# Gate-build look-ahead of a ten-stage fp32 network: one step per four tokens, 45 units ahead, three loads ahead earlier, and a step between query and scores

## Chip, cores and metric

The kernel runs on one core of a Trainium2 chip. The metric is the device time of one execution, in microseconds, as the median of several runs. A profile of one further execution supplies the trace.

## The reference, cut to what matters

Ten stages run one after the other on 256 tokens of width 1024, all in fp32. Two of them (`p0` and `p1`, one in each layer of the first block) are a routed feed-forward with 16,384 experts per layer. Both are the same code; the change is in them alone.

```python
q = (xb @ w_q).reshape(n, 8, 2, 128)                    # 8 heads, two half-queries each
s = einsum('nhpc,pkc->nhpk', q, subkeys)                # scores against 128 keys per half
sv, si = top_k(s, 16)
cand = sv[:, :, 0, :, None] + sv[:, :, 1, None, :]      # 16 x 16 candidates
fv, fi = top_k(cand.reshape(n, 8, 256), 16)
eid = ...                                               # si0 * 128 + si1 of the 16 winners
gw = softmax(fv)
act = gelu(einsum('nhkd,nd->nhk', u_tab[eid], xb))
y = einsum('nhkd' , (gw * act), v_tab[eid])             # sum over heads and winners
```

The other eight stages (an mLSTM mixer, an RG-LRU mixer, four gated feed-forwards, an S5 mixer, a convolution mixer) are not touched.

## The kernel before

**Dense instead of gathered.** The kernel does not gather expert rows. It multiplies all 256 tokens with all 16,384 rows of `u` and of `v`, and puts a gate matrix in between that is zero for experts a token did not choose. `u` and `v` are cut into 64 units of 256 experts (1 MB each). Every fp32 product is three fp32r matmuls (high x high, low x high, high x low), so each unit is split after its load: ScalarE copies the high part (line 217, tile `uwh` or `vwh`), VectorE subtracts to get the low part (line 218, `uwl` or `vwl`).

**Stages of a peer block.** In the order of the program:

- *Route* (`route`): projects the queries (256 columns of `w_q` per head), scores them (`psc`, line 909, copied to `sc`), takes the top 16 twice on VectorE (lines 661 to 672), decodes the winners (`decode`) and turns weights and indices into the rows `sel` (`selection`).
- *Gate build* (`build_gates`): makes the gate matrix for eight tokens at a time, `n` = 0 to 31. VectorE writes four one-hot tiles `oh` of 128x1024 (lines 1026 and 1028), TensorE multiplies them in two groups of eight small matmuls into `pG` (lines 1039 and 1040, one group per four tokens), ScalarE copies each group into `stg` (line 1042), and every 16 tokens a 1 MB store takes `stg` to `gd` in DRAM (line 1045, ScalarE's queue; `stg` has two buffers). Below, a *half* is one of the 64 passes of its inner loop: four tokens, two one-hots, one group.
- *Drain*: the rest of the look-ahead, with nothing else beside it.
- *y loop*: 64 passes over the units of `v`; each loads and splits a unit of `v`, multiplies the activations by the gates (`gt`, loaded from `gd`), splits them (`pch`, `pcl`), and runs 24 matmuls of 512 columns into the four banks `py`. From pass `LOOK - 3` on, each pass also computes one more unit of `u`.

**The look-ahead.** Activations gelu(u x) don't depend on the routing, so `ahead()` is a generator that works on units of `u` while route and gate build go on. One *step* is a `next(gen)`: 12 matmuls of 256 columns into `pP`, and at every second step the split of half a unit that the matmuls reach four steps later (128x1024 elements on ScalarE, then the same on VectorE). Four steps are one unit; a gelu ends it. `LOOK` units are made this way. The first 15 stay in SBUF (`lact`); those after them are spilled to DRAM (`ad`, line 733, 0.25 MB each, on SyncE's queue) and recalled in the y loop (line 741), except the last three (`pact`).

Where the steps go is written out by hand. `tick(cost, rate)` in `route` adds cost times rate to a credit and runs a step for each whole credit. In `build_gates` each half adds `RATE[3]` and runs at most one step:

```python
one_hot(n + 1, coming, (2 * g, 2 * g + 1))
credit += RATE[3]
if credit >= 1.0:
    credit -= 1.0
    next(gen, None)
gates(n, oh, g)
```

Ahead of the loop come four one-hots for the first eight tokens with three steps between them. By the credits, 97 steps are run before the loop, 57 in it, and the rest of the 160 in the drain.

**Order.** In `route` the instructions of TensorE, VectorE and ScalarE keep the order of the program (`in_order`); in `build_gates` SyncE's do too. Each engine's queue is then fixed, and an instruction that waits holds up those behind it. Loads and spills share SyncE's queue. `depth[0]` says how many units past the current one have been issued for loading: 1 in `route`, 3 in the build (`DEP`); three `raw` buffers hold them.

**Query and scores.** `project(h)` is a generator that `route` advances twice per pass of `candidates`: two empty advances, the first half of the projection (24 matmuls), the second half with the copy to `pq` (line 888, ScalarE), one more empty advance, then the scores `psc`, which read `pq`.

Of the kernel before, what the change touches and what calls it, by code (L numbers as in the profile page):

```python
# [35 lines left out]
S5S = ("00001111",) + ("01010101",) * 3  # L36
S5O = "s0 s1; s2 s3|y0 y1; t0 t1 s4 s5|w2 g0 g1 w3 y2 y3; t2 t3 s6 s7|g2 g3 y4 y5; t4 t5|y6 g4 y7 t6 g5 t7 g6 g7"
DEP = (1, 3)
RATE = (2.0, 0.66, 1.33, 0.9)
SPN = 3  # L40
LPN = 1
IOR = ("tensor","vector","scalar")
# [1 line left out]
NX = (4, 2, 2, 2)  # L44
FILL = (3,) * 20
LATE = (3, 4)
LOOK = 40
TAIL = (9, 1)
PARTS = (4, 4) + (2,) * 40
MAGIC = 12582912.0  # L50
# [7 lines left out]
class K:  # L58
# [615 lines left out]
    def peer(self, x, xt, nxt, i):  # L674
        nc, a, tc = self.nc, self.a, self.tc
        HOLD, KEEP = 15, 3
        with ExitStack() as st:
# [3 lines left out]
            gd = self.dram.tile([P, 16, P, 16], F32, name=f"gd{i}")  # L681
            ad = self.dram.tile([P, max(1, LOOK - KEEP - HOLD), 2, S], F32, name=f"ad{i}")
            sel = [lpool.tile([P, S], F16, name=f"sel{j}") for j in range(4)]
# [31 lines left out]
            def u_mm(q, s):  # L715
# [8 lines left out]
                if s == 3:  # L724
                    if q < HOLD:
                        ac = lpool.tile([P, 2, S], F32, name="lact", tag="lact", bufs=HOLD)
                    elif q < LOOK - KEEP:
                        ac = top.tile([P, 2, S], F32, name="spact", tag="spact", bufs=2)
                    else:
                        ac = top.tile([P, 2, S], F32, name="pact", tag="pact", bufs=KEEP + 2)  # L730
                    nc.scalar.activation(ac, ps.rearrange("p (k s) -> p k s", k=2), AF.Gelu)
                    if HOLD <= q < LOOK - KEEP:
                        nc.sync.dma_start(ad[:, q - HOLD], ac)
# [4 lines left out]
            def recall(q):  # L738
                if HOLD <= q < LOOK - KEEP:
                    acts[q] = top.tile([P, 2, S], F32, name="spact", tag="spact", bufs=2)  # L740
                    nc.sync.dma_start(acts[q], ad[:, q - HOLD])

            def v_load(q):
# [4 lines left out]
                if q == 62:  # L748
                    raw = slots["r"][0].rearrange("p (k n) -> p k n", k=2)
                    vst[q] = [raw[:, k:k + 1] for k in range(2)]  # L750
                elif q > LOOK - KEEP:
                    vst[q] = [self.res.tile([P, 1, D], F32, tag="v", name="vraw", bufs=2) for _ in range(2)]
# [36 lines left out]
            def ahead():  # L789
                u_load(0)  # L790
                for s in range(4):
                    u_split(0, s)
                n = 0
                for q in range(LOOK):
                    while n < min(q + depth[0], LOOK):
                        n += 1
                        u_load(n)
                    for s in range(4):
                        u_split(q + 1, s)
                        u_mm(q, s)  # L800
                        yield

            depth = [DEP[0]]
            gen = ahead()
            with tc.tile_pool(name="route", bufs=1) as pool:
                self.route(pool, xt, i, sel, gen)
            with tc.tile_pool(name="build", bufs=1) as pool:
                depth[0] = DEP[1]
                with self.in_order(True, None, IOB):
# [43 lines left out]
            nxt.load()  # L853
            return self.residual_ln(x, banks, g, b, nxt)

    def route(self, pool, xt, i, sel, gen):
        nc, a = self.nc, self.a
        sk = pool.tile([P, 2, P], F32, name="sk")
        nc.sync.dma_start(sk, a["peer_subkeys"][i].rearrange("h k c -> k h c"))
# [14 lines left out]
        def tick(cost, rate):  # L874
            credit[0] += cost * rate
            while credit[0] >= 1.0:
                credit[0] -= 1.0
                next(gen, None)

        def weights(h):  # L880
            if h < 8:
                raw = self.ring.tile([P, 2048], F32, tag="raw", name="raw").rearrange("p (k n) -> p k n", k=8)
                nc.sync.dma_start(raw, a["peer_w_q"][i][:, h * 256:h * 256 + 256].rearrange("(p k) c -> p k c", k=8))
                units[h] = raw

        def query(h, ps):
            heads[h] = pool.tile([P, 2, S], F32, name="pq", tag="pq", bufs=2)
            nc.scalar.activation(heads[h], ps.rearrange("p (f s) -> p f s", f=2), AF.Copy)

        def project(h):  # L890
            if h >= 8:
                return
            yield
            yield
            if h >= 2:
                w = units.pop(h)
                ps = self.mmb()
                for f in range(2):
                    self.feat(ps[:, f * S:(f + 1) * S], w, f * P, (f + 1) * P, xt)
                    if f == 0:  # L900
                        yield
                query(h, ps)
            yield
            yield
            qT = heads.pop(h)
            pss = self.acc("psc")
            for t in range(2):
                for f in range(2):
                    nc.tensor.matmul(pss[:, (2 * t + f) * P:(2 * t + f + 1) * P], qT[:, f, t * P:(t + 1) * P],
                                     skT[:, f, :], start=True, stop=True)  # L910
            sc[h] = pool.tile([P, 4, P], F32, name="sc", tag="sc", bufs=2)
            nc.scalar.activation(sc[h], pss.rearrange("p (f s) -> p f s", f=4), AF.Copy)

        def candidates(h):
            for t in range(2):
                self.top16(*((sc[h][:, 2 * t + f, :], sv[t][:, h, f, :], si[t][:, h, f, :]) for f in range(2)))
                yield 2.0
            cds = []
            for t in range(2):
                cd = pool.tile([P, 112], F32, name="cd", tag="cd", bufs=2)  # L920
                for c0, a0, na, nb in ((0, 0, 4, 16), (64, 4, 12, 4)):
                    nc.vector.tensor_tensor(cd[:, c0:c0 + na * nb].rearrange("p (a b) -> p a b", a=na),
                                            sv[t][:, h, 0, a0:a0 + na, None].to_broadcast([P, na, nb]),
                                            sv[t][:, h, 1, None, 0:nb].to_broadcast([P, na, nb]), ALU.add)
                cds.append((cd, fv[t][:, h, :], fp[t][:, h, :]))
            yield 0.6
            self.top16(*cds)
            yield 2.0
# [36 lines left out]
        for _ in project(0):  # L965
            tick(1.0, RATE[0])
        with self.in_order(True, None, IOR):
            late = iter(())
            for h in range(8):
                ahead = project(h + 1)  # L970
                for n, cost in enumerate(candidates(h)):
                    next(ahead, None)
                    if n == LPN:
                        weights(h + 2)
                    tick(cost, RATE[1])
                    next(ahead, None)
                    if n == SPN and h + 2 in units:
                        units[h + 2] = self.split(units[h + 2], 8, 256)
                        tick(2.2, RATE[1])
                    if h >= 4:  # L980
                        d = next(late, None)
                        if d is not None:
                            tick(d, RATE[2])
                for _ in ahead:
                    pass
                if h == 3:
                    late = decode(slice(0, 4))
            for late in (late, decode(slice(4, 8))):
                for cost in late:
                    tick(cost, RATE[2])  # L990
            self.selection(pool, mk, gen, sel, fv, ix)
# [25 lines left out]
    def build_gates(self, pool, sel, gd, gen):  # L1017
# [3 lines left out]
        def one_hot(n, oh, js):  # L1021
            for j in js if n < 32 else ():
                o = pool.tile([P, 4, P, 2], F16, name=f"oh{j}", tag=f"oh{j}", bufs=2)
                sc = sel[j][:, n * 8:n * 8 + 8].rearrange("p (g t) -> p g t", g=4)[:, :, None, :].to_broadcast([P, 4, P, 2])
                if j < 2:
                    nc.vector.tensor_tensor(o, self.iota2[:, None].to_broadcast([P, 4, P, 2]), sc, ALU.is_equal)
                else:
                    nc.vector.tensor_tensor(o, oh[1], sc, ALU.mult)
                oh.append(o)
# [23 lines left out]
        for n in range(32):  # L1053
            for g in range(2):
# [3 lines that stand above are left out]
# [707 lines left out]
```

## Time and profile before

| what | value |
|---|---|
| median of 3 runs | 3032.01 us (3028.15 to 3034.11) |
| profiled execution | 3031.37 us |
| its span in the trace | 3029.7 us |
| TensorE matmul busy | 2939.7 us (97%) |
| TensorE weight load busy | 2684.8 us (89%) |
| VectorE busy | 2052.3 us (68%) |
| ScalarE busy | 1571.9 us (52%) |
| mean DMA rate | 205 GB/s |

Busy shares are averages over all ten stages. The page's matmul ends are modelled, so a busy TensorE is not one at its peak; idle time of an engine counts only where it holds up the one that sets the end. Times of the trace are counted from the start of the span.

### The profile page before, as it was taken

How to read it: one execution, taken by the hardware profiler on the slowest of the kernel's cores; microseconds unless marked ns; L12 is line 12 of the kernel's file. 1: busy time of each engine (PE TensorE's matmuls, PEld its weight loads, DVE VectorE, ACT ScalarE, POOL GpSimd, SP SyncE). 2: the span in 40 equal slices, each digit the busy share in tenths (PEclk: the TensorE clock that was granted, in tenths of full speed). 3: DMA queues.
4: the chain of work that ended last, by engine and by line, in shares of the span. 5: the costliest groups of instructions: out<-in, count | busy, mean ns of one | idle time of the engine just before them, and what ended most of it. 6: DMA issues, size and time to landing. Idle time of an engine off the chain costs nothing. (4 is left out here: it accounts for less than half of the span.)

```text
span 3029.7 us, 48905 instructions
## 1 busy us (share of the span) xinstructions
PE 2939.7 (97%) x20062; PEld 2684.8 (89%) x20062; DVE 2052.3 (68%) x3516; ACT 1571.9 (52%) x2180; POOL 10.9 (0%) x18
## 2 busy tenths in 40 slices
PE   9999999999999999989999999999899999999999
PEld 8899898888999889989888899899888999998898
DVE  5678897565555778989666555677776455479554
ACT  4544486444444664468444444456835454466544
POOL 0000000000000000000000000000000000000000
PEclk9999999999999999999999999999999999999999
DMA  7355489785665644568877565566864565552353
GB/s 235 126 169 181 171 293 311 239 286 188 222 210 181 216 155 154 181 226 298 271 268 257 182 222 197 194 200 225 297 226 165 180 206 178 173 169 98 126 192 128
DMA packets 332220, 620.70 MB, mean 205 GB/s; under 512 B 32444, under 2 KB 243292, under 8 KB 310493
## 3 DMA queue, kind: packets, MB, share of 16 engines
q1 hardware_dynamic: 327389, 584.03, 58.0%
q10 hardware_dynamic: 4608, 33.56, 2.7%
q8 instruction: 157, 2.57, 0.3%
q14 instruction: 66, 0.54, 0.1%
HBM read 557.77 MB, written 59.77 MB: 204 GB/s over the span
## 5 line engine op out<-in xcount | busy, mean ns | idle before, releaser
L218 DVE TENSOR_TENSOR wl<-raw,wh 128x1024 fp32r<-128x1024 f32 (+1 forms) x440 | 481.1, 1123 | 165.1 <-ACT wh L217 164.1
L217 ACT ACTIVATE wh<-raw 128x1024 fp32r<-128x1024 f32 (+1 forms) x440 | 411.4, 974 | 172.8 <-PE py L154 47.9
L152 PE MATMUL pP<-xth,uwh 128*128 128x256 f32 x1664 | 485.2, 292 | 1.0 <-ACT uwh L217 1.0
L154 PE MATMUL pP<-xth,uwl 128*128 128x256 f32 x1664 | 473.0, 284 | 1.8 <-DVE uwl L218 1.8
L153 PE MATMUL pP<-xtl,uwh 128*128 128x256 f32 x1664 | 472.7, 284 | 0.0
L152 PE MATMUL pf<-xth,wh 128*128 128x256 f32 x1280 | 363.1, 284 | 1.3 <-ACT wh L217 1.3
L154 PE MATMUL pf<-xth,wl 128*128 128x256 f32 x1280 | 362.9, 284 | 0.0
L153 PE MATMUL pf<-xtl,wh 128*128 128x256 f32 x1280 | 362.6, 283 | 0.0
L154 PEld LDWEIGHTS pP<-xth,uwl 128*128 128x128 f32 x1664 | 320.7, 193 | 2.7 <-DVE uwl L218 2.6
L152 PEld LDWEIGHTS pP<-xth,uwh 128*128 128x128 f32 x1664 | 320.9, 193 | 2.2 <-ACT uwh L217 1.2
L153 PEld LDWEIGHTS pP<-xtl,uwh 128*128 128x128 f32 x1664 | 321.3, 193 | 1.1
L152 PE MATMUL py<-vwh,pch 128*128 128x512 f32 x800 | 315.9, 395 | 2.0 <-ACT pch L217 2.0
L153 PE MATMUL py<-vwl,pch 128*128 128x512 f32 x800 | 315.8, 395 | 1.5 <-DVE vwl L218 1.4
L154 PE MATMUL py<-vwh,pcl 128*128 128x512 f32 x800 | 315.2, 395 | 0.0
L152 PEld LDWEIGHTS pf<-xth,wh 128*128 128x128 f32 x1280 | 245.3, 192 | 4.6 <-ACT wh L217 1.6
L153 PEld LDWEIGHTS pf<-xtl,wh 128*128 128x128 f32 x1280 | 245.5, 192 | 2.3
L218 DVE TENSOR_TENSOR uwl<-raw,uwh 128x1024 fp32r<-128x1024 f32 x164 | 199.4, 1220 | 69.9 <-ACT uwh L217 68.0
L154 PEld LDWEIGHTS pf<-xth,wl 128*128 128x128 f32 x1280 | 245.5, 192 | 0.6 <-DVE wl L218 0.4
L218 DVE TENSOR_TENSOR vwl<-raw,vwh 128x2048 fp32r<-128x2048 f32 x76 | 174.2, 2292 | 82.7 <-ACT vwh L217 82.5
L217 ACT ACTIVATE uwh<-raw 128x1024 fp32r<-128x1024 f32 x164 | 169.9, 1057 | 39.6 <-DMA raw<-in_peer_u 14.4
L152 PEld LDWEIGHTS py<-vwh,pch 128*128 128x128 f32 x800 | 150.8, 188 | 36.8 <-ACT pch L217 2.8
L153 PEld LDWEIGHTS py<-vwl,pch 128*128 128x128 f32 x800 | 150.7, 188 | 36.4 <-DVE vwl L218 2.3
(558 smaller groups left out, 6536.0 us busy)
## 6 DMA issues: line engine op xcount, KB each, us to landing
raw<-in_ffn_w SPq DMA_DIRECT2D x132, 1024.0 KB, 5.3
raw<-in_peer_u SPq DMA_DIRECT2D x82, 1024.0 KB, 5.5
raw<-in_peer_v SPq DMA_DIRECT2D x76, 1024.0 KB, 5.0
vraw<-in_peer_v SPq DMA_DIRECT2D x100, 512.0 KB, 3.9
sraw<-in_peer_u SPq DMA_DIRECT2D x46, 1024.0 KB, 7.5
gd<-stg ACTq DMA_DIRECT2D x32, 1024.0 KB, 6.0
gt<-gd SPq DMA_DIRECT2D x32, 1024.0 KB, 7.3
raw<-in_peer_w_q SPq DMA_DIRECT2D x16, 1024.0 KB, 5.5
```

The source lines that it names most:

```text
L152: mm(out, sh, mh, start=start, stop=False)
L153: mm(out, sh, ml, start=False, stop=False)
L154: mm(out, sl, mh, start=False, stop=stop)
L217: self.nc.scalar.activation(h, src, AF.Copy)
L218: self.nc.vector.tensor_tensor(low, src, h.bitcast(F32), ALU.subtract)
```

## The change

Four constants and lines move:

1. `RATE[3]`, the credit per half of the gate build, goes from 0.9 to 1.2.
2. `LOOK` goes from 40 to 45 units.
3. `depth` is handed to `route`, which sets it to 3 at `h == 6`, the seventh head, instead of at the start of the build.
4. In pass `n == 1` of a head both advances of `project` come ahead of the load of weights and of the look-ahead steps, where one came before and one after. So both halves of the projection and the query's copy stand together, and the steps of that pass fall between the copy and the scores.

```diff
-RATE = (2.0, 0.66, 1.33, 0.9)
+RATE = (2.0, 0.66, 1.33, 1.2)
...
-LOOK = 40
+LOOK = 45
...
-                self.route(pool, xt, i, sel, gen)
+                self.route(pool, xt, i, sel, gen, depth)
...
-    def route(self, pool, xt, i, sel, gen):
+    def route(self, pool, xt, i, sel, gen, depth):
...
             for h in range(8):
                 ahead = project(h + 1)
+                if h == 6:
+                    depth[0] = DEP[1]
                 for n, cost in enumerate(candidates(h)):
                     next(ahead, None)
+                    if n == 1:
+                        next(ahead, None)
                     if n == LPN:
                         weights(h + 2)
                     tick(cost, RATE[1])
-                    next(ahead, None)
+                    if n != 1:
+                        next(ahead, None)
```

## Rows read from the trace of the kernel before

**Rows 1.** Waits of TensorE's matmuls over the whole span: us in total, times, longest.

```profile
PE pG L1039 <- DVE oh L1028: 14.4, 7, 3.5
...
PE pG L1040 <- DVE oh L1028: 4.2, 12, 0.4
PE psc L909 <- ACT pq L888: 4.1, 6, 0.7
...
PE pP L154 <- DVE uwl L218: 1.8, 4, 0.7
```

**Rows 2.** Stretches: length, busy us (count) by engine, clock, DMA share, GB/s.

```profile
171.73:363.39 191.66, 187.22 (x1550) 185.56 (x1550) 162.73 (x566) 87.41 (x107) 0.00 (x0) 1.00 0.48 168
363.39:497.19 133.80, 123.23 (x1201) 118.33 (x1199) 116.18 (x160) 103.01 (x111) 0.00 (x0) 0.95 0.81 284
497.19:512.49 15.30, 14.26 (x121) 14.06 (x119) 7.22 (x6) 6.81 (x8) 0.00 (x0) 1.00 1.03 333
512.49:719.27 206.78, 206.72 (x888) 167.25 (x889) 130.86 (x110) 88.45 (x73) 0.00 (x0) 1.00 0.79 260
...
1313.25:1446.16 132.91, 120.40 (x1199) 115.58 (x1198) 116.34 (x160) 102.81 (x111) 0.00 (x0) 0.97 0.80 286
1446.16:1461.40 15.24, 14.32 (x122) 14.11 (x119) 7.21 (x6) 6.86 (x8) 0.00 (x0) 1.00 0.96 319
...
360.00:380.00 20.00, 15.39 (x105) 14.51 (x105) 14.08 (x23) 8.21 (x10) 0.00 (x0) 0.74 0.45 171
```

**Rows 3.** The same view: seven undisturbed halves of the build, and the drain.

```profile
469.81:483.48 13.67, 13.67 (x142) 13.37 (x141) 12.36 (x17) 11.75 (x13) 0.00 (x0) 1.00 0.90 341
...
497.30:511.00 13.70, 13.70 (x117) 13.70 (x116) 5.81 (x3) 6.02 (x6) 0.00 (x0) 1.00 1.01 340
```

**Rows 4.** Gate matmuls of p0, then of p1: duration, first and last start.

```profile
L1039 PE MATMUL pG<-oh,oh x256: 218/218/330, 366.0 to 497.1; 128*128 128x128 f16 x128
...
L1039 PE MATMUL pG<-oh,oh x256: 217/218/330, 1315.9 to 1446.1; 128*128 128x128 f16 x128
```

**Rows 5.** Waits of TensorE's matmuls, build and drain of p0.

```profile
PE pG L1039 <- DVE oh L1028: 6.6, 4, 2.4
...
PE py L152 <- ACT pch L217: 1.0, 1, 1.0
```

**Rows 6.** The same for p1, up to 1481 us.

```profile
PE pG L1039 <- DVE oh L1028: 7.8, 3, 3.5
...
PE py L153 <- DVE vwl L218: 1.4, 1, 1.4
```

**Rows 7.** Timelines of SyncE's queue, ScalarE and VectorE at p0's build start.

```profile
349.49 15.05 SPq L733 DMA_DIRECT2D ad<-spact  x3
364.63 1.35 SPq L704 DMA_DIRECT2D raw<-in_peer_u  x3
...
370.47 1.06 ACT L217 ACTIVATE uwh<-raw 128x1024 fp32r<-128x1024 f32 x1 [6.28 <-DMA raw<-in_peer_u]
...
371.56 1.23 DVE L218 TENSOR_TENSOR uwl<-raw,uwh 128x1024 fp32r<-128x1024 f32 x1 [5.07 <-ACT uwh L217]
```

**Rows 8.** Timeline of VectorE in the undisturbed halves.

```profile
475.35 1.22 DVE L218 TENSOR_TENSOR uwl<-raw,uwh 128x1024 fp32r<-128x1024 f32 x1 [1.09 <-ACT uwh L217]
476.49 1.28 DVE L1026 TENSOR_TENSOR oh<-iota,sel 128x1024 f16<-128x1024 f16 x2
...
479.02 1.22 DVE L218 TENSOR_TENSOR uwl<-raw,uwh 128x1024 fp32r<-128x1024 f32 x1
```

**Rows 9.** Groups of instructions of p0's build: busy us, mean ns, idle before.

```profile
L1026 DVE TENSOR_TENSOR oh<-iota,sel 128x1024 f16<-128x1024 f16 x62 | 39.9, 684 | 0.6 <-PE pG L1040 0.6
...
L218 DVE TENSOR_TENSOR uwl<-raw,uwh 128x1024 fp32r<-128x1024 f32 x31 | 37.8, 1223 | 16.3 <-ACT uwh L217 15.5
```

**Rows 10.** Waits of VectorE in p0's route.

```profile
DVE uwl L218 <- ACT uwh L217: 18.5, 10, 3.1
```

**Rows 11.** Stores of `stg` in p0's build: issue to landing.

```profile
DMA to landing us min/median/max: 5.7/6.0/9.4
```

## Prediction

> **What bounds the kernel now.** TensorE does, nearly everywhere, so the question is where it still loses time. I read the waits of its matmuls over the span first [rows 1]: the longest entry that the change can reach is the gate matmul waiting for a one-hot, 14.4 us in seven waits, with 4.2 us more in twelve short ones right behind. Then the stretches [rows 2]. In route TensorE is idle for 4.4 of 191.66 us. In the two builds it is idle for 10.6 of 133.80 and 12.5 of 132.91 us, and its granted clock is 0.95 and 0.97 there, 1.00 in the others: pieces at the lower of the two levels (1.2 of 2.4 GHz) come with its waits (0.74 in the 20 us around the build's start) and cost 0.05 x 133.8 = 6.7 and 0.03 x 132.9 = 4.0 us of full speed. In the y loop (512.49 on) it is busy for 206.72 of 206.78 us: nothing to gain. So the two builds, with the turn into the y loop (1.0 us idle at 497.19:512.49), hold about 35 us of loss.
>
> Why TensorE waits in the build: VectorE. It makes two one-hots a half whether or not TensorE got a step. After every tenth half, where the credit of 0.9 pays none, the next group comes after 0.5 instead of 2 us, and TensorE then waits for one-hots. The biggest waits stand at the start. The one of 2.4 us in p0 is for the first four one-hots; the one of 3.5 us in p1 [rows 5, 6] comes a few halves on, from late loads, as p0 shows: SyncE's queue has three spills in a row from 349.49 us, each waiting for its gelu; the next three loads come out only at 364.63 us; ScalarE waits 6.28 us for the first, and VectorE 5.07 us behind it [rows 7].
>
> With steps in every half the build runs smoothly: from 469.81 to 483.48 us there are seven halves, 142 matmuls (7 x 20 and two of the borders), TensorE busy throughout: 1.953 us a half [rows 3]. In the drain 117 matmuls take 13.70 us, 1.41 us per step of twelve [rows 3].
>
> **The change, part by part.**
>
> *1.2 instead of 0.9.* The code pays at most one step per half, so 1.2 acts as 1.0: 64 steps in the loop, not 57, none skipped, and not the 77 that 1.2 would say. The first half gets one as well. That step goes ahead of the first gate group, into the wait from 363.39 to 366.0 us [rows 4], which its one-hots set.
>
> I cost the stretch from the last step ahead of the loop to the first y matmul, for equal content. Before, p0: 133.80 + 15.30 = 149.10 us, holding 64 groups, 57 steps and 117/12 = 9.75 steps of the drain. After: 2.6 us to the first group, 63 halves x 1.953 = 123.0, the last group 0.5, and the 66.75 - 64 = 2.75 steps still missing x 1.41 = 3.9: 130.0 us. That is 19.1 us less. p1: 132.91 + 15.24 = 148.15 us, 18.1 less. Sum 37.2 us, before stalls. Checked from the other side, idle (10.6 + 1.0) and clock (6.7) of p0 make 18.3.
>
> What each of the others has to do per two halves, 3.91 us of TensorE: VectorE four one-hots and one split, 3.67 us from one split to the next where nothing holds it (475.35 to 479.02) [rows 8]. It fits, with 6% to spare. But its splits waited for ScalarE: 16.3 us before 31 of them [rows 9], of which 5.07 at the start [rows 7], so 0.36 us each. 3.67 + 0.36 = 4.03, 0.12 over, x 32 = 4 us per build if all of it returns; nothing if it stays in the slack, as in the seven halves, which contain a wait of 1.09 us and lost nothing. I take 3 us per build, nearer the upper end, because no stretch shows 64 halves in a row: 6 us.
>
> *45 units.* Steps are moved, not added: 4 x 45 = 180 in all, 19 left for the drain instead of 6, and five units fewer beside the y loop. A unit there costs what it costs in the drain, nothing to gain. Five more units per block are spilled and recalled, ten transfers of 0.26 MB; they lie beside the y loop's matmuls, at a DMA share of 0.79 and 260 GB/s [rows 2]. With that cover gone, 10 x 1.0 us per block. What it does bring: the first y matmul waits 1.0 us for `pch` behind the gate reload in p0 [rows 5], already in the 149.10, and in p1 one waits 1.4 us for a split of `v` [rows 6]. A drain of some 27 us (19 x 1.41) hides reload and loads: 1.4 us more.
>
> *Three loads ahead from the seventh head.* The loads for the build's start go out three units, twelve steps, earlier, past the spills. The 6.28 us wait [rows 7] should go. Its price is inside the 37.2; if the part fails, VectorE starts late by 5 us and the early halves stall as before: +2 to +4 us a block. It issues no transfer more than before.
>
> *Query and scores.* `psc` waits six times 0.69 us for the copy `pq`: 4.1 us [rows 1]. After, 1.32 + 0.40 steps' credit stands between, one or two steps, 1.4 to 2.8 us of matmuls, so the wait goes. Against it: `pq` now stands ahead of that pass's splits in ScalarE's queue, and it waits for 24 more matmuls, some 2.8 us; VectorE's low part waits behind. In p0's route VectorE has 18.5 us of such waits [rows 10] to absorb that, though not in the late part, where TensorE waits for it (`uwl`, 1.8 us in four) [rows 1]. Bounds: 4.1 us gained, or per block 2.8 lost at the last head against 2.1 gained, 1.4 lost in all. I take 2.0 us gained, nearer the gain, since five of the six heads have the slack.
>
> Sum: 37.2 + 1.4 + 2.0 - 6 = 34.6 us. The profiled execution took 3031.37 us, so 2996.8; the median of the runs stands 0.6 above it: 2997.
>
> One rule of the Trainium skill speaks against this. A pair of one-hots takes 1.28 us where one alone has 0.684 [rows 8, 9]: the second starts before the recorded end of the first. "VectorE: DVE Perf Modes", section "The DRAIN you can't avoid", says that the next operation does not start until the pipe has emptied; by it, recorded durations could not overlap. By that, VectorE would need 4 x 0.684 + 1.223 = 3.96 us per two halves, over TensorE's 3.91, and the sum would lose 2 x 1.7 us more; by the row it has slack. The row decides.
>
> **The rivals.**
>
> *VectorE becomes the bound.* For it: 3.67 against 3.91 us is close, and waits on ScalarE come on top. At the worst, durations that don't overlap and a wait at each split: 3.96 + 0.36 = 4.32, 0.41 over, x 32 = 13 us per build where I took 3: 3017. Against it: the seven halves at full TensorE. Middle 3007. The skill's rule alone would be its mildest form, 3000 us; the rows contradict it, and it gets 0.02 of this rival's chance.
>
> *The clock falls as before.* If the shorter wait at the start and new ones still bring down the granted clock, 6.7 + 4.0 = 10.7 us stay lost: 3008. For it: p0's clock fell with no wait of a gate matmul longer than 2.4 us [rows 5]. Against it: the waits behind skipped steps are gone with the skips.
>
> *The steps are only moved.* TensorE counts 97% busy already; if the seven extra steps lengthen the build by what they save in the drain, nothing is left: 3028 to 3034. Against it: 23 us of idle in the builds [rows 2].
>
> *Slower: the transfers set the pace.* Per four halves one unit of `u` (1.05 MB), one store (1.05 MB) and one spill (0.26 MB) must move, 2.36 MB, and two `stg` buffers let ScalarE wait for a store. At 1.953 us a half that is 302 GB/s. The gain is gone when a half takes 1.953 + 18.6/63 = 2.25 us, that is when DMA gives less than 262 GB/s; at 240 GB/s a half takes 2.46 us and the kernel 3057. For it: stores landed after up to 9.4 us [rows 11], more than the 7.8 us of four halves, at a share of 0.81. Against it: the seven halves moved 341, the drain 340 GB/s [rows 3].
>
> **How the numbers follow.** Forecast 0.58 (own range 2988 to 3004), VectorE 0.18, clock 0.12, only moved 0.07, transfers 0.05. The lower bound: all of 37.2 + 1.4 + 4.1 without stalls, 2989, rounded to 2988. The upper, 3014, takes in the clock and most of VectorE's cases. 0.2%, 6 us, is about what a measurement of this kernel can tell from no change. Faster 0.88 (the first three), same 0.07, slower 0.05.
>
> **What the profile after would show.** In both builds, groups of gate matmuls every 1.95 us, no pair without a step between, 64 steps; the gate matmul's waits for one-hots down from 18.6 to below 6 us in all; build stretch about 126 to 129 us with more matmuls in it (some 1,280, where 1,200 are now), clock 0.98 or more. ScalarE's wait for `raw` at the build's start gone, the loads' issue ahead of the last spills. `psc` not among the waits. First y matmul without a wait, some 32 us after the last gate group if the next unit's four steps still go ahead of it as now (9.75 steps, where 6 were left), 27 if not. Route within 2 us of 191.66.
>
> The prediction is wrong if the half settles above 2.05 us (VectorE or DMA waits at each split), if the y loop is no longer without gaps (spills, or the first fresh unit late at pass 42), or if the route grows.

## The result and the profile after

The changed kernel takes 2996.91 us (median of four runs, 2995.42 to 2998.97) where the kernel before takes 3030.08 (four runs, 3027.47 to 3034.11): ratio 0.9896 [0.9884, 0.9908], faster by 33.2 us. Forecast was 2997.0. The profiled execution took 2995.42 us, its span is 2993.7. So the total is right; its terms are not all, and the largest error is one of sign. That the total came out within 0.1 us is luck: errors of opposite sign cancel, as the terms below show.

In the new line numbers everything behind the changed loop of `route` moves down by five: one-hots are lines 1031 and 1033, gate matmuls 1044 and 1045. The waits of TensorE's matmuls over the whole span (us in total, times, longest) that answer to [rows 1], and one that was small before:

```profile
PE py L153 <- DVE vwl L218: 6.2, 4, 2.7
...
PE pG L1044 <- DVE oh L1033: 1.9, 2, 0.9
...
PE pP L154 <- DVE uwl L218: 1.8, 4, 0.7
...
PE pG L1045 <- DVE oh L1033: 0.6, 2, 0.3
```

Waiting for one-hots went from 18.6 to 2.5 us. `psc` is not in the list any more. New at the top of the waits that the change touches: the y loop's matmuls wait for the split `vwl`. The stretches that answer to [rows 2] (length, busy us and count of TensorE, its weight loads, VectorE, ScalarE, GpSimd, then clock, DMA share, GB/s): route, build, drain and the first 12 us of the y loop of p0; then build, drain and y start of p1.

```profile
171.67:361.90 190.23, 187.86 (x1561) 186.81 (x1562) 163.92 (x568) 88.58 (x109) 0.00 (x0) 1.00 0.52 179
361.90:487.07 125.17, 123.94 (x1272) 120.91 (x1270) 118.70 (x160) 105.08 (x113) 0.00 (x0) 1.00 0.80 296
487.07:514.75 27.68, 27.67 (x232) 27.47 (x230) 16.10 (x17) 14.42 (x18) 0.00 (x0) 1.00 0.86 295
514.75:527.00 12.25, 8.76 (x33) 6.57 (x32) 6.46 (x7) 4.83 (x4) 0.00 (x0) 0.87 1.13 345
...
1299.39:1424.56 125.17, 123.94 (x1271) 120.91 (x1270) 118.72 (x160) 105.06 (x113) 0.00 (x0) 1.00 0.80 297
1424.56:1451.99 27.43, 27.43 (x233) 27.43 (x230) 17.26 (x17) 14.32 (x18) 0.00 (x0) 1.00 0.91 318
1451.99:1464.00 12.01, 9.78 (x43) 7.64 (x42) 5.74 (x7) 4.83 (x4) 0.00 (x0) 1.00 1.12 340
```

Both builds take the same 125.17 us, with 71 matmuls more than p0's had in 133.80, at clock 1.00. The fourth and the last row are the surprise: TensorE is idle for 3.5 and 2.2 us where [rows 2] show p0's y loop without gaps. The gate matmuls, against [rows 4], still have the pace of the undisturbed halves in [rows 3]: 123.9 us from the first to the last.

```profile
L1044 PE MATMUL pG<-oh,oh x256: 217/218/234, 363.1 to 487.0; 128*128 128x128 f16 x128
```

SyncE's queue at the build's start, against [rows 7]. Two of the three loads now go out from 347.34 us on, ahead of the two last spills, and the third at 362.40, where all three came out at 364.63 before. ScalarE's wait for `raw` is gone.

```profile
347.34 7.20 SPq L704 DMA_DIRECT2D raw<-in_peer_u  x2
354.86 6.77 SPq L733 DMA_DIRECT2D ad<-spact  x2
362.40 0.33 SPq L704 DMA_DIRECT2D raw<-in_peer_u  x1
```

The same queue at the end of the drain, and VectorE's timeline there:

```profile
499.56 0.53 SPq L760 DMA_DIRECT2D gt<-gd  x1
500.14 2.32 SPq L733 DMA_DIRECT2D ad<-spact  x1
502.57 10.20 SPq L756 DMA_DIRECT2D raw<-in_peer_v  x3
512.82 0.53 SPq L760 DMA_DIRECT2D gt<-gd  x1
```

```profile
507.01 1.90 DVE L774 TENSOR_TENSOR lact<-lact,gt 128x512 f32<-128x512 f32 x3 [5.38 <-DMA gt<-gd]
...
510.02 2.35 DVE L218 TENSOR_TENSOR uwl<-raw,uwh 128x1024 fp32r<-128x1024 f32 x2
...
513.62 2.29 DVE L218 TENSOR_TENSOR vwl<-raw,vwh 128x2048 fp32r<-128x2048 f32 x1
520.94 1.29 DVE L774 TENSOR_TENSOR lact<-lact,gt 128x512 f32<-128x512 f32 x2 [5.03 <-DMA gt<-gd]
522.15 2.28 DVE L218 TENSOR_TENSOR vwl<-raw,vwh 128x2048 fp32r<-128x2048 f32 x1
```

The gate reload waits 6.9 us for the last store of the gates, and the first loads of `v` stand behind it in SyncE's queue: they go out from 502.57 us on, where before they did from 490.92, ahead of the first y matmul by 12 us instead of 22. On VectorE two products `lact` of a later pass, which wait 5.03 us for their gates, stand ahead of the split `vwl` that TensorE needs now. The two queues hold each other: products that wait 5.38 us for the first reload also stand ahead of the last splits of `u` (`uwl`, 510.02 us). Those splits free the `raw` buffer that the third load of `v` waits for (8.8 us in SyncE's queue), and the second reload stands behind that load and goes out only at 512.82 us.

### The profile page after: what moved, and what is told of

Same layout as the page of the kernel before. It is cut to its first block, busy times and chain, and to the rows that moved or that the text cites. A ratio compares the mean times of both kernels' runs of the same rounds, so it can differ in the third digit from the quotient of the medians.

```text
span 2993.7 us, 48914 instructions
## 1 busy us (share of the span) xinstructions
PE 2924.5 (98%) x20062; PEld 2672.5 (89%) x20062; DVE 2054.0 (69%) x3506; ACT 1570.9 (52%) x2170; POOL 10.9 (0%) x18
## 5 line engine op out<-in xcount | busy, mean ns | idle before, releaser
L152 PE MATMUL pP<-xth,uwh 128*128 128x256 f32 x1760 | 509.9, 290 | 0.0
L154 PE MATMUL pP<-xth,uwl 128*128 128x256 f32 x1760 | 497.4, 283 | 1.8 <-DVE uwl L218 1.8
L153 PE MATMUL pP<-xtl,uwh 128*128 128x256 f32 x1760 | 497.0, 282 | 0.0
L153 PE MATMUL py<-vwl,pch 128*128 128x512 f32 x848 | 336.4, 397 | 6.2 <-DVE vwl L218 6.2
L154 PE MATMUL py<-vwh,pcl 128*128 128x512 f32 x848 | 335.9, 396 | 0.0
L152 PE MATMUL py<-vwh,pch 128*128 128x512 f32 x848 | 335.7, 396 | 0.0
L218 DVE TENSOR_TENSOR uwl<-raw,uwh 128x1024 fp32r<-128x1024 f32 x184 | 223.2, 1219 | 54.7 <-ACT uwh L217 50.9
L218 DVE TENSOR_TENSOR vwl<-raw,vwh 128x2048 fp32r<-128x2048 f32 x86 | 197.0, 2291 | 77.9 <-ACT vwh L217 77.7
L217 ACT ACTIVATE uwh<-raw 128x1024 fp32r<-128x1024 f32 x184 | 191.0, 1059 | 13.9 <-PE pP L153 9.0
L154 PEld LDWEIGHTS py<-vwh,pcl 128*128 128x128 f32 x848 | 160.3, 189 | 38.0
```

The source lines that it names most:

```text
L152: mm(out, sh, mh, start=start, stop=False)
L153: mm(out, sh, ml, start=False, stop=False)
L154: mm(out, sl, mh, start=False, stop=stop)
L217: self.nc.scalar.activation(h, src, AF.Copy)
L218: self.nc.vector.tensor_tensor(low, src, h.bitcast(F32), ALU.subtract)
```

## The experiments

Each ratio is to the kernel before as it ran beside these kernels (median 3025.7 us for the first four, 3029.8 for the next four, 3028.76 for the last four), with its 95% interval. Edits are to the changed kernel unless said.

**The four parts undone, one at a time.**

```diff
-RATE = (2.0, 0.66, 1.33, 1.2)
+RATE = (2.0, 0.66, 1.33, 0.9)
```

> The changed kernel with the credit per half back at 0.9 (45 units, early loads and moved query kept). Theory: the skipped halves are what TensorE loses time by, so the waits for one-hots behind each tenth half return (six per build, about 1.4 us at every other one, 0.3 us at the others, 2 us at the last), with pieces at the lower clock: 6 to 9 us per block, 3010 to 3015 us. The early loads still save the wait for the first unit. Rival, the early loads made the gain and the rate did little: within 3 us of the changed kernel's 2997. Rival, the steps are only moved: also 2997, as seven more steps would go to the drain at the same price.

Measured: 3012.75 us, 0.9954 [0.9941, 0.9968], as expected. The waits for one-hots are back, also behind the halves without a step (waits in p0, then the build's stretch and the start of the y loop):

```profile
PE pG L1044 <- DVE oh L1033: 5.7, 4, 2.4
PE pG L1045 <- DVE oh L1033: 1.9, 6, 0.4
```

```profile
361.60:488.50 126.90, 119.01 (x1203) 114.79 (x1204) 115.54 (x159) 102.73 (x110) 0.00 (x0) 0.99 0.78 282
...
513.00:530.00 17.00, 17.00 (x124) 16.12 (x124) 11.87 (x13) 7.29 (x7) 0.00 (x0) 1.00 1.09 353
```

The stretch is 1.7 us longer than 125.17 with some seven steps fewer in it, which then make the drain 37 us long; from the last step ahead of the loop to the first y matmul that costs 10.5 (p0) and 12.2 us (p1). In return the y loop starts without a gap (second window row) and is 6.9 and 4.1 us shorter than the changed kernel's. So the rate alone is worth more than the ratio says: part of its gain is handed back at the y loop's start.

```diff
-LOOK = 45
+LOOK = 40
```

> The changed kernel with 40 units again: 97 + 63 steps use up the look-ahead, and no drain is left. Theory: the first y matmul comes no earlier than 15.3 us behind the start of the last gate group (store, reload, product, split), as in the kernel before; only the four steps of one more unit can stand in that time, so TensorE idles some 9 us per block: 3010 to 3016 us. Rival, the drain hides nothing that counts, since the y loop's start is set by its own loads: within 3 us of 2997, or less, as the changed kernel loses 6 us at the start of the y loop.

Measured: 3015.29 us, 0.9965 [0.9953, 0.9977], as expected. A wait and a stretch of p0:

```profile
PE py L152 <- ACT pch L217: 13.8, 1, 13.8
```

```profile
487.00:512.00 25.00, 11.23 (x69) 9.46 (x68) 9.63 (x13) 5.71 (x7) 0.00 (x0) 0.73 0.84 267
```

With 40 units the 160 steps are used up when the loop ends. The chain from the last gates to the first y matmul (store, reload, product, split) then stands bare: 13.8 us of waiting. The five units are the cover of that chain.

```diff
-                if h == 6:
-                    depth[0] = DEP[1]
```

> The changed kernel with one load ahead in the whole route. Theory: ScalarE again waits some 6 us for the first unit of the build, VectorE 5 us behind it, and the first halves stall by 2 to 4 us per block, with a lower clock there: 3001 to 3007 us. Rival, with a step in every half TensorE never runs ahead of VectorE, the slack of 6% takes the late start up, and nothing is lost: 2996 to 2999 us.

Measured: 3008.6 us, 0.9945 [0.9931, 0.9958]. The same two builds take 132.10 and 130.75 us instead of 125.14 (from the start of the last step matmul ahead of the first group to the start of the last gate matmul), all of it lost at the start. Waits of ScalarE and TensorE, then the start and the rest of the build:

```profile
ACT uwh L217 <- DMA raw<-in_peer_u: 6.1, 1, 6.1
...
PE pG L1042 <- DVE oh L1031: 5.0, 2, 4.1
```

```profile
363.40:380.00 16.60, 10.98 (x85) 10.09 (x84) 11.57 (x17) 7.25 (x8) 0.00 (x0) 0.79 0.77 285
380.00:490.00 110.00, 110.00 (x1131) 107.59 (x1129) 103.60 (x140) 93.11 (x99) 0.00 (x0) 1.00 0.80 298
```

Three spills stand ahead of the loads again (348.08 to 363.15 us). VectorE's slack does not absorb the 6.1 us, and the clock falls as it did before. I had said 2 to 4 us a block; it is 7.0 and 5.6.

```diff
-                    if n == 1:
-                        next(ahead, None)
...
-                    if n != 1:
-                        next(ahead, None)
+                    next(ahead, None)
```

> The changed kernel with the query's copy again right ahead of the scores. Theory: six waits of 0.69 us return, and as VectorE's late part starts behind the scores of the last head, most of it reaches the end: 2999 to 3001 us. Rival, VectorE's decode sets the end of the route and swallows it: 2997 us, with TensorE's wait for the gates' weights shorter by as much.

Measured: 3002.94 us, 0.9921 [0.9906, 0.9935], a little more than expected. By the trace, route loses 2.8 us a block (189.97 us against 187.15 from the first step on). The timeline of TensorE shows why a wait recorded with 0.69 us costs more than that (start, length, then the instruction):

```profile
208.17 0.28 PE L153 MATMUL mmb<-xtl,wh 128*128 128x256 f32 x1
208.29 0.28 PE L154 MATMUL mmb<-xth,wl 128*128 128x256 f32 x1
209.25 0.94 PE L909 MATMUL psc<-skT,pq 128*128 128x128 f32 x6 [0.69 <-ACT pq L888]
```

Matmuls start every 0.12 us but are shown 0.28 long. From the last start to the start of `psc` are 0.96 us, 0.84 more than the usual 0.12. Three such waits a block are 2.5 us, most of the 2.8.

The four undone parts lose 0.0058, 0.0069, 0.0049 and 0.0025 against the changed kernel's 0.9896: together 0.0201, where the whole change gains 0.0104. The parts lean on each other.

**The rate alone, on the kernel before.** Only `RATE[3]` goes to 1.2 there.

> The kernel before with 1.2 alone (40 units, one load ahead in route, query next to scores). Theory: 63 of the 160 steps go into the build and none are left for the drain, so the first y matmul waits for the gates' reload as with 40 units in the changed kernel (17 to 18 us behind the last group), and the first unit's late load still stalls the start: of the 35 us that the builds gave, some 8 to 12 are left, 0.996 to 0.9975 of the kernel before. Rival, the rate alone brings the gain: 0.991 or less.

Measured: 3034.94 us, 1.0024 [1.0013, 1.0035]: slower, though its twelve runs spread from 3029.01 to 3041.66. I missed the sign, for the reason that 40 units had already shown (waits, then the stretch at the end of p0's build):

```profile
PE py L152 <- ACT pch L217: 13.9, 1, 13.9
...
PE pG L1039 <- DVE oh L1028: 4.6, 2, 3.6
```

```profile
497.10:515.40 18.30, 4.38 (x40) 4.18 (x37) 3.72 (x4) 4.21 (x5) 0.00 (x0) 0.75 1.01 316
```

The build does 86 matmuls more in the same 133.7 us, and the drain of 15.3 us is replaced by 18.3 us of almost nothing. The start still stalls, because the loads still come late. A steady rate is worth nothing until there are units for the drain and loads for the start.

**The start of the y loop.** Once more the changed kernel, and beside it one where VectorE and SyncE keep the program's order through the drain and the first 12 passes of the y loop, with the first two loads of `v` ahead of the gate reload.

> The changed kernel once more, as the measure for the runs beside it. Theory: 0.9896 of the kernel before, give or take 0.001, with waits of 3 to 7 us at the start of the y loop in one or both blocks.

Measured: 2995.9 us, 0.9890 [0.9875, 0.9904], with waits for `vwl` of 3.4 us in p0 and 2.4 in p1.

```diff
+YORD = 12
...
+            with self.in_order(True, early, ("vector", "sync")):
...
+                v_load(0)
+                v_load(1)
                 g_load(0)
...
-                with self.in_order(fresh, order):
+                with self.in_order(fresh or q < YORD, ...):
```

> The changed kernel with the order of the program kept on VectorE and SyncE in the drain and the first twelve passes of the y loop, and the first two loads of v ahead of the first reload of the gates. Theory: the waits at the start of the y loop (3.5 us of idle and 3.4 us of clock in the first block, 2.7 us in the second) come from VectorE's queue, where products for later passes wait for a reload ahead of the low part of v, and from v's loads held up behind the reload; in order they go: 0.9896 - 0.003 = 0.9866 of the kernel before, about 9 us under the changed kernel. Rival, the transfers themselves are too slow there (345 GB/s, share 1.13, in those 12 us): the same waits stand elsewhere in the stretch, within 3 us of the changed kernel.

Measured: 2990.96 us (2987.52 to 2991.94), 0.9870 [0.9855, 0.9884]; none of its runs is as slow as the fastest of the changed kernel beside it (2995.25). The waits for `vwl` are gone. The gain beside the changed kernel is 4.9 us where 9 were expected, and the trace shows where a part of it goes: the kept order itself costs time. The first twelve passes take 69.2 us in either block, the next twelve of p0, in free order, 66.9. To see which queue it was, VectorE's order alone, with the reload ahead of `v`'s loads as in the changed kernel:

> The changed kernel with the order of the program kept on VectorE alone at the start of the y loop; the reload of the gates stays ahead of v's loads. Theory, if VectorE's queue is the cause: as with both, 0.987 of the kernel before and no wait for the low part of v above 1 us. Rival, v's loads behind the reload are the cause: 0.989, with the waits still there.

Measured: 2989.76 us, 0.9883 [0.9867, 0.9899]. This interval takes in both 0.987 and 0.989, so the time doesn't decide between the theory and its rival; the trace does. The first 12.25 us of the y loop of p0, first with both orders, then with VectorE's alone:

```profile
515.45:527.70 12.25, 12.25 (x56) 9.79 (x55) 7.81 (x7) 5.83 (x6) 0.00 (x0) 1.00 0.94 286
```

```profile
515.08:527.33 12.25, 12.25 (x52) 9.49 (x53) 7.67 (x7) 6.02 (x6) 0.00 (x0) 1.00 0.82 268
```

SyncE's queue with VectorE's order alone:

```profile
502.20 5.32 SPq L757 DMA_DIRECT2D raw<-in_peer_v  x3
507.57 0.52 SPq L761 DMA_DIRECT2D gt<-gd  x1
```

TensorE has no gap in either version. The first load of `v` goes out as late as in the changed kernel (502.20 against 502.57 us), so that delay alone does no harm. The third load and the second reload do come earlier (507.57 against 512.82 us), though nothing in SyncE's order ahead of them was changed: VectorE's splits free the buffers sooner. So the trace puts the wait down to VectorE's queue, where products of later passes stand ahead of the splits. The times of the two versions can't be told apart.

**More units.**

```diff
-LOOK = 45
+LOOK = 47
```

> The changed kernel with 47 units instead of 45, nothing else. Theory: with the credit back at 0.9 a drain of 26 steps, 37 us, had no wait at the y loop's start, so 27 steps here, 38 us, should leave the last store, the reload and v's loads the time they need: 0.987 of the kernel before, 6 to 9 us under the changed kernel. Rival, the order in VectorE's queue is at fault whatever the drain's length: within 3 us of the changed kernel.

Measured: 2987.78 us (2986.90 to 2991.16), 0.9867 [0.9852, 0.9881], as expected. The first y matmuls wait 1.0 us once in p0 and 0.6 us once in p1; the row of p0:

```profile
PE py L153 <- DVE vwl L218: 1.0, 1, 1.0
```

Eight more steps in the drain (39.0 us instead of 27.7 from the last gate matmul to the first y matmul in p0) give the loads and the reload time to land, with no order changed. Both remedies together:

> 47 units and the order of the program at the start of the y loop together. Theory: both take away the same waits, so they do not add up: 0.9865 of the kernel before, at most 2 us under the run with 47 units. Rival, they add up: 0.984.

Measured: 2987.85 us, 0.9875 [0.9860, 0.9890]. They don't add up: 47 units leave little of the wait that the order removes, and the first twelve passes again take 69.2 and 69.5 us, so the order's own price is paid.

**1.2 paid in full.** A half runs as many steps as the credit allows, and 50 units keep the drain at 27 steps.

```diff
-LOOK = 45
+LOOK = 50
...
-                if credit >= 1.0:
+                while credit >= 1.0:
```

> The credit paid out in full: 'while' instead of 'if', so that 1.2 is 77 steps in the build, and 50 units, which leaves a drain of 26 steps, one less than with 47 units. Theory: at one step per half TensorE has no free time left in the build, so thirteen more steps lengthen it by 13 x 1.41 = 18 us per block and shorten what comes later by as much: 0.9867 of the kernel before, within 0.001 of the run with 47 units. Rival, the build still has room: up to 37 us less.

Measured: 2988.53 us, 0.9869 [0.9854, 0.9884], no better than 47 units at one step a half. The gate matmuls:

```profile
L1044 PE MATMUL pG<-oh,oh x256: 218/218/233, 364.3 to 505.4; 128*128 128x128 f16 x128
```

They take 141.1 us instead of 123.9. The loop holds 76 steps (I had said 77), twelve more, at 17.2/12 = 1.43 us each: the price of a step in the drain. TensorE is full; at one step a half there is no room left for a step that costs less. The run also bounds what a longer drain is worth. It has the 27 steps and 39.0 us of the run with 47 units, but in p0 the y loop still waits, as products that wait for their gates again stand ahead of a split:

```profile
PE py L153 <- DVE vwl L218: 2.5, 1, 2.5
```

So the length of the drain does not settle it by itself. That the order in VectorE's queue is the cause here too is read from the trace alone; no run keeps the order with 50 units.

**VectorE's slack.** One more one-hot tile of the same size every eight tokens, read by nobody.

```diff
+                if g == 0:
+                    extra = pool.tile([P, 4, P, 2], F16, name="extra", tag="extra", bufs=1)
+                    nc.vector.tensor_tensor(extra, ..., ALU.is_equal)
```

> The changed kernel with one more one-hot of 128x1024 per eight tokens on VectorE, which nothing reads. Theory: VectorE needs 3.67 us per two halves and TensorE 3.91, so VectorE has 0.24 us to spare; 0.605 more makes it the bound, with 4.28 us per two halves, 12 us more per build: 0.997 of the kernel before. Rival, VectorE has more room than its queue shows: 0.989 to 0.991.

Measured: 3014.2 us, 0.9958 [0.9945, 0.9972]. The gate matmuls, the busy times in the build, then VectorE's timeline over two halves:

```profile
L1044 PE MATMUL pG<-oh,oh x256: 217/219/234, 363.1 to 494.4; 128*128 128x128 f16 x128
```

```profile
380.00:490.00 110.00, 108.24 (x1063) 102.30 (x1063) 110.00 (x160) 88.89 (x94) 0.00 (x0) 1.00 0.76 288
```

```profile
475.45 1.21 DVE L218 TENSOR_TENSOR uwl<-raw,uwh 128x1024 fp32r<-128x1024 f32 x1
...
477.79 0.67 DVE L1063 TENSOR_TENSOR extra<-iota,sel 128x1024 f16<-128x1024 f16 x1
...
479.59 1.21 DVE L218 TENSOR_TENSOR uwl<-raw,uwh 128x1024 fp32r<-128x1024 f32 x1
```

The build grows by 131.3 - 123.9 = 7.4 us, where I had said 12. VectorE is now the bound: it is busy for all of the 110 us where TensorE idles for 1.8, at 479.59 - 475.45 = 4.14 us per two halves. With 0.60 us for one more one-hot (a pair takes 1.28, one alone 0.68 [rows 8, 9]), its need without it is 3.54 us, not 3.67: the slack is 0.37 of 3.91 us, 9% and not 6%.

## Why the prediction was right, term by term

**Build and drain, predicted 37.2 less 6, measured 35.7: right, without the reserve.** I compare equal content, from the last step ahead of the loop to the first y matmul. p0: 1.44 + 125.17 + 27.68 = 154.29 us with 64 + 19 = 83 steps, less the 83 - 66.75 = 16.25 steps that the kernel before did not have there, at 1.44 us: 130.9, where 149.10 stood. That is 18.2 us (19.1 predicted); p1 17.5 (18.1 predicted). The working was right in each step: 1.2 acts as 1.0, 64 steps, every half 1.95 us, clock 1.00. What it lacks to 37.2 is 0.5 us a block in the first half, which takes 2.4 us, and 0.1 to 0.4 in the drain, whose steps take 1.44 to 1.46 us and not 1.41. The 6 us that I kept for VectorE's waits on ScalarE were not needed: those waits went from 15.5 us in 14 (the idle time before the 31 splits was 16.3) to 2.1 us in 13, none over 0.2. They came from the halves without a step and from the late loads: with the credit undone they are 15.9 us, with the depth undone 10.4.

**Start of the y loop, predicted 1.4 gained, measured some 8 lost: wrong.** The step that failed is "A drain of some 27 us (19 x 1.41) hides reload and loads". The drain was as long as said, and it did hide the reload for the first pass; but I took the order of the queues behind it for that of before. The waits are 3.5 us (p0) and 2.7 us (p1); in p0 the clock is 0.87 over the 12.25 us and 0.99 over the next 173, some 1.6 + 1.7 = 3.3 us more. These 9.5 us stand where the kernel before had the 1.4 that was to be gained, so 8.1 were lost. The run with VectorE in the program's order shows the cause. A longer drain can hide it (47 units) but need not (2.5 us with 50 units and the same drain).

**Route, predicted 2.0, measured 5.8: mis-sized.** 190.23 us hold one step of 1.44 more than 191.66 did: 2.9 us a block. I had 4.1 as the most to gain, from six waits of 0.69 us; each costs 0.85 from start to start, which makes 5.1; where the other 0.7 comes from is not traced. And the late part did not lose anything: TensorE's wait for `uwl` is the same 1.8 us in four as in [rows 1].

Sum: 35.7 + 5.8 - 8.1 = 33.4 us, and the medians differ by 33.2. The reserve that was not needed and the larger route cancelled the y loop's start. The sum is a microsecond high: from the start of route to the end of the y loop p0 took 830.6 us and now takes 816.1, p1 831.0 and 813.2, together 32.3 less. The profiled spans differ by 36.0 us; the rest lies in stages that the change does not touch. Those behind p1 give 5.7 (from 1952.60 us on the kernel before took 1077.00 us; the same 7,163 matmuls now take 1071.30), and those between the blocks take 2.1 back (119.28 us before, 121.37 now, at a granted clock of 1.00 and 0.99).

**The rivals.** *VectorE as the bound* fell: no wait for it behind the first half. It is the next bound, 0.37 us away per two halves. The rule that I named from the Trainium skill ("VectorE: DVE Perf Modes", section "The DRAIN you can't avoid") was read too strictly: the same section adds that a next operation which is not held starts earlier. The trace agrees with that: with the extra one-hot, five one-hots and a split have recorded durations of 5 x 0.673 + 1.206 = 4.57 us and recur every 4.14, so they overlap. *The clock falls as before* fell in the builds (1.00), and came true on a small scale in p0's y loop. It does come back when the loads are late (0.79 in 363.40:380.00 with the depth undone). *The steps are only moved* fell: the same content takes 18 us less. But with the rate alone it is what happens: there 1.2 moves the loss from the halves to the loop's end. *The transfers* fell: 296 GB/s in the build at no loss; stores landed after at most 7.9 us.

**The signs.** 1,272 gate and step matmuls in the stretch (1,280 said), 125.17 us (a little under the 126 to 129 said), first y matmul 27.7 us behind the last group (27 or 32 said), waits for one-hots 2.5 us (below 6 said), `raw` and `psc` gone: as said. "First y matmul without a wait" held too; the gaps come a few matmuls later. So one of the three signs of being wrong did come, "if the y loop is no longer without gaps", by neither of the causes named beside it (spills, a late fresh unit). The other two did not.

## What to carry to other kernels

A look-ahead has to last until the chain behind the loop has come through: work that fills the loop better takes its cover from what follows, so raise the amount together with the rate (the rate alone made this kernel 0.24% slower, with five more units and earlier loads it is 1.04% faster, with seven 1.33%). More units are no safe cure for a queue in the wrong order, though, and keeping the program's order has a price of its own (2.3 us in twelve passes here). When a change shifts the moment at which a queue's waits end, read the order of every queue behind it again, VectorE's and SyncE's too: a product that waits for its reload held the split that was due. And keep a reserve only for a wait whose cause stays.

## What the runs showed of the hardware

A wait that the profile records as 0.69 us cost 0.84 to 0.85 us, because a matmul's modelled end reaches 0.16 us past the start of the next (0.28 long, one every 0.12). Bare waits also cost clock beyond their own length: around a wait of 13.9 us the granted clock is 0.75 in 497.10:515.40, and waits of no more than 4.1 us at a build's start come with 0.79 in 16.6 us; so part of these stretches ran at the lower of the two levels, and 3.5 us of waits in p0's y loop came with 0.87 where p1, with 2.7 us, shows 1.00.
